# Zero-padded scan products, channel-major attention values and a new order for a hybrid decoder layer on one core

## The chip, the core and the metric

The kernel runs on one core of a Trainium2 chip. The core has five engines with a queue of instructions each: TensorE (PE in the profile; its weight loads are listed apart as PEld), VectorE (DVE), ScalarE (ACT), GpSimd (POOL) and SyncE (SP), whose queue starts the transfers. An engine works through its queue in order, and the engines wait for one another by semaphores. Matmuls read SBUF and write PSUM. The metric is the device time of one execution in microseconds (us); lower is better.

## The reference

One layer over 512 tokens of 1024 channels. What matters here are two mixers that run on the same projection of the normalized input.

```python
P = h @ W_in                       # attention q/k/v, scan inputs, gate logits
# attention: groups of (window, dilation); per head the groups are
# weighted by their softmax denominators (lse)
wts = softmax(stack(lses), axis=0)
y_att = sum(wts[..., None] * stack(outs), axis=0) @ W_att_out
# RWKV-7: for every token, with a 64x64 state for each of 16 heads
sa = state @ aa_t
state = state * w_t + sa * bb_t + v_t * k_t
y_t = state @ r_t
# then
x = x + gate1 * ((sig(g_att) * y_att + sig(g_rwkv) * y_rwkv) @ W_o)
x = x + gate2 * ConvFFN(adaLN(RMSNorm(x), c))
out = RMSNorm(x)
```

The conditioning vector `c` gives six rows of scales, shifts and gates: `c @ w_ada + b_ada`.

## The kernel before

Nearly all large products are made in three passes, as high times high, high times low and low times high parts of weights and activations. A weight block is loaded into a `raw` tile (two buffers), ACT copies its high part to `whi` (L1141, L193), DVE subtracts to get `wlo` (L1144, L194), and TensorE then runs 512-column matmuls (all through the helper at L148; transposes at L151). In the trace a product of plain 32-bit operands is two matmul instructions with two weight loads, so the counts of small products there are twice those of the calls.

**A planner sets the order.** From the start to the end of the scan (about 0 to 750 us) the order of each engine's queue isn't the order of the code. `Plan.add` takes a task with its engine, an estimated time, a priority, what it depends on, which buffers it takes and gives, and a `lag`: a time for which, after the engine is free again, the task's result and buffers still count as not there. `Plan.run` simulates all engines with these estimates and issues the tasks in the simulated order. On the chip each engine follows that order, however long things really take. Large projections (`body`, one task for each matmul) have low priority and fill TensorE between other tasks.

**Attention (`attention`, L672).** In two halves of four heads, first for the group with dilation 1 (`gi` 0), then for the group with dilation 4 (`gi` 1). `attend` (L788) goes through blocks of 128 queries of a pair of heads: `scores` on TensorE, `stat` (mask and minimum) on DVE, `exp` on ACT, `turn` (transposes) on TensorE, `turned` (copy to `pts`, two buffers), `values` (L831) on TensorE into `po`, and `out` (L841), a copy to `o[gi]`. There are 28 blocks with two key blocks and 4 with one. `values` makes tokens the rows of the result: the probabilities are the stationary operand (128x128), and 64 columns of the values move. When all is done, the two groups' shares are worked out (`diff`, `exps`, `share`, L1000 to L1013), `scale` (L1015) multiplies the rows of `o` by them, `turn` transposes the two groups into the same PSUM tile so that they add up, ACT copies it (L1034) and SP stores it to `att_d`. The second group's tokens are interleaved by 4, and the transposes write them back in order. Only when all these tasks are done is the memory of the next stage opened (`opened`).

**Conditioning (`ada_rest`, L328).** Four of the six rows are made in the same stretch: 8 loads of 512 KB each into `araw` (two buffers), 8 multiply-adds on DVE into `acc` (L345, L347), and then small matmuls named `ada` that sum over the rows of `acc`.

**Scan.** Sixteen heads go in four groups `g` of two pairs. `pair` (L1228) makes keys, rates and so on of two heads, `inverse` (L1441) or `inverse16` (L1577) solves a group's triangular blocks, and `chain` (L1745) carries the state through eight blocks `c` of 64 tokens. A chain step has these groups on TensorE: `state` (L1798), that is `xy<-mbd,ar` (for `c` > 0) and then four products `xy<-uv,gt` over the 64 rows of one half; `state_out`, `xo<-mbd,ar`; `solve`, `u<-xs,gt`; `update`, `u<-uv,bkt`; and `outs`, `xo<-uv,gt`. Every second block, `vals` adds `u<-cen,v` and two ACT copies into `uv`. `inverse` inverts 32x32 blocks on DVE in 14 double and 3 single steps; `inverse16` inverts 16x16 blocks in 6 double and 3 single steps, and joins them with two TensorE passes (`half_pe`, L1679) of 64 products of 32x32 tiles each. Groups 0 to 2 use `inverse`, group 3 `inverse16`. Memory for the pairs of group `g` is that of group `g`-2.

**Output product (`rwkv_out`, L2098).** Behind the plan comes code in program order. `rwkv_out` goes through eight blocks `m` of output channels, each 24 matmuls `pr` (blocks 0 to 2 have 18 of them done ahead). The weights of blocks 3 and 4 are loaded ahead, those of 5 to 7 when the block two before is done. In the same loop DVE and ACT mix the branches (`mhi`, `mlo`), and one row block of `w_o` is loaded and split in each turn, through the same two `raw` buffers. Then come the product with `w_o` (`mix_out`, matmuls `o`) and the gated MLP.

Of the kernel before, what the change touches and what calls it, by code (L numbers as in the profile page):

```python
# [10 lines left out]
F32 = mybir.dt.float32  # L11
F32R = mybir.dt.float32r
# [6 lines left out]
P = 128  # L19
S = 512  # L20
# [108 lines left out]
class Layer:  # L129
# [198 lines left out]
    def ada_rest(self):  # L328
# [5 lines left out]
        for part, name in ((2, "gt1"), (3, "sh2"), (4, "sc2"), (5, "gt2")):  # L334
            d, prev = {}, None
            for k in range(KD):
                def load(k=k, d=d, part=part):
                    d["raw", k] = self.accp.tile([P, D], F32, tag="araw", name=self.n("araw"), bufs=2)
                    nc.sync.dma_start(d["raw", k], self.w_ada[0][k * P : (k + 1) * P, part * D : (part + 1) * D])

                def step(k=k, d=d):
                    raw, ck = d["raw", k], self.col["c"][:, k : k + 1]
                    if k == 0:
                        d["acc"] = self.accp.tile([P, D], F32, tag="acc", name=self.n("acc"), bufs=2)
                        nc.vector.tensor_scalar(d["acc"], raw, ck, 0.0, op0=ALU.mult, op1=ALU.add)  # L345
                    else:
                        nc.vector.scalar_tensor_tensor(d["acc"], raw, ck, d["acc"], op0=ALU.mult, op1=ALU.add)  # L347
# [324 lines left out]
    def attention(self):  # L672
# [4 lines left out]
        o = [ap.tile([P, 4, ATT_W], F32, name="o0"), None]  # L677
# [110 lines left out]
        def attend(gi, hf, order, blocks, width, mask, V, ready, prio):  # L788


            last, pos, scs = {0: [], 1: []}, {}, []
            S0, E0 = S_ + prio, E_ + prio
            for n, i, new, end in order:
# [37 lines left out]
                def values(n=n, i=i, d=d, new=new, end=end):  # L831
                    if new:
                        pos[n] = self.aps.tile([P, 256], F32, tag="po", name=self.n("po"), bufs=2)
                    vs = V(n)
                    for h in range(2):
                        cs = slice(i * P + h * 64, i * P + h * 64 + 64)
                        for j, v in enumerate(vs):
                            self.mm(pos[n][:, cs], d["pts"][:, h, j * P : (j + 1) * P], v[:, cs],
                                    new and h == 0 and j == 0, end and h == 1 and j == len(vs) - 1)

                def out(n=n, i=i, new=new):  # L841
                    c0, c1 = (i * P if new else 0), i * P + P
                    if gi and o[1] is None:
                        o[1] = ap.tile([P, 4, ATT_W], F32, tag="o1", name="o1")
                    nc.scalar.copy(o[gi][:, n, hf * 256 + c0 : hf * 256 + c1], pos[n][:, c0:c1])
# [11 lines left out]
                t = pe(0.9 * wd / 256, values, [t], S0, take=("po",) if new else (), give=("pts",), name="po")  # L857
                last[i].append(t)
                if end:
                    first = gi and not outs[gi]  # L860
                    outs[gi].append(sca(0.37, out, [t], E0, take=("o1",) if first else (), give=("po",), name="o"))
# [106 lines left out]
        for _ in ada:  # L968
            pass

# [23 lines left out]
        scaled = []  # L994
        for gi in range(2):
# [19 lines left out]
            def scale(n, gi=gi, ea=ea):  # L1015
                ov = o[gi][:, n, :].rearrange("p (h e) -> p h e", h=8)
                nc.vector.tensor_tensor(ov, ov, ea[:, n, :].unsqueeze(2).to_broadcast([P, 8, 64]), op=ALU.mult)
            t = dve(0.6, diff, [got[gi], *stats[gi]], name="al")
            t = sca(0.45, exps, [t], name="al")
            t = dve(1.2, share, [t], name="al")  # L1020
            scaled += [dve(0.7, lambda n=n, scale=scale: scale(n), [t, *outs[gi]], name="al") for n in range(4)]
        for i in range(4):
            d = {}

            def turn(i=i, d=d):
                d["pa"] = self.aps.tile([P, S], F32, tag="pt", name=self.n("pa"), bufs=2)
                for n in range(4):
                    self.tr(d["pa"][:, n * P : (n + 1) * P], o[0][:, n, i * P : (i + 1) * P], n == 0, False)
                for n in range(4):
                    self.tr(d["pa"][:, n::4], o[1][:, n, i * P : (i + 1) * P], False, n == 3)  # L1030

            def out(d=d):
                d["t"] = self.awl.tile([P, S], F32, tag="attT", name=self.n("attT"), bufs=2)
                nc.scalar.copy(d["t"], d["pa"])  # L1034
            t = pe(0.95, turn, scaled, take=("pt",), name="pa")
            t = sca(0.6, out, [t], take=("attT",), give=("pt",), name="pa")
# [540 lines left out]
    def inverse16(self, g):  # L1577
# [101 lines left out]
        def half_pe(j):  # L1679

            if j == 0:
                d["pe"] = self.cps.tile([P, 512], F32, tag="t", name=self.n("pe"))
            for y in range(16):
# [61 lines left out]
    def chain(self, g):  # L1745
# [24 lines left out]

        def value(c, x):
            if x == 0:
                uvs[c] = cw.tile([P, 2, 256], F32, tag="uv", name=self.n("uv"), bufs=2)
# [9 lines left out]
        def vals(c):  # L1783
            t = pe(0.54, lambda: values(c), [start, last_uv])
            t = sca(0.38, lambda: value(c, 0), [t], C_, take=("uv",))
            uvd[c] = uvd[c + 1] = sca(0.38, lambda: value(c, 1), [t], C_)
        vals(0)
        for c in range(NCH):
# [9 lines left out]
            def state(c=c, s=s, gt=gt, R=R, X=X, ih=ih):  # L1798
# [4 lines left out]
                for i, h, cs, ci in ih:  # L1803
                    self.mm(xy[X[i], cs], gt(i, h, R[i], X[i]), s["uv"][R[i], ci], c == 0 and h == 0, h == 1)
# [45 lines left out]
            st = pe(0.6 if c else 0.33, state, [uvd[c], start] + mb, take=("xy",), name=f"xy{g}.{c}")  # L1850
            so_ = pe(0.33 if c else 0.0, state_out, [st], C_ + 0.01, take=("xo",), name="xo")
# [246 lines left out]
    def rwkv_out(self, mpool, wpool, psp):  # L2098
# [16 lines left out]
        for m in range(KD):  # L2115
# [3 lines left out]
            if 2 < m < KD - 2:  # L2119
                ahead.append(block(m + 2))  # L2120
# [284 lines left out]
```

## Time and profile before

| | |
|---|---|
| three runs | 1211.57, 1217.01, 1217.90 us (median 1217.01) |
| profiled execution | 1212.94 us, span 1211.2 us |
| mean granted TensorE clock | 0.993 |
| TensorE instructions | 7456 matmuls, 7456 weight loads |
| ACT / POOL instructions | 1014 / 228 |
| DMA | 138.39 MB, mean 114 GB/s |

The profile is of one execution. A row of the timeline has the start of an instruction (or of a run of like ones), its time, the engine, the line, the operation, the tile written and the tiles read, the shapes and the count; a bracket gives the idle time before it and what ended it. For matmuls the shapes begin with the rows and columns of the array that are in use, as in 128*64. A matmul's own time is its latency; how often one can start is seen from the next start. A row of a group has the count, the busy time and the mean of one in ns, then the idle time before it. In rows of waits the three numbers are the total, how often, and the longest.

### The profile page before, as it was taken

Reading aid. Unit: us, or ns where it says so; the run is one execution under the profiler, and the core shown is the slowest. Engines: PE = TensorE matmul, PEld = TensorE weight load, DVE = VectorE, ACT = ScalarE, POOL = GpSimd, SP = SyncE. Lnnn points to the kernel's source line nnn. Section 1 sums busy time; section 2 is a strip of 40 time slices with the busy share of each in tenths; the row PEclk is TensorE's granted clock in tenths of the full one; section 3 lists DMA queues with packets and bytes.
Section 4 is the critical chain, followed back from the end, with each engine's and each line's share of the span. In section 5 each row is a group of like instructions: output and inputs, shape, how many; then the busy total and the mean of one; then the engine's idle time right before and its main releaser. Section 6 shows DMA issues by size and latency. Waiting matters only on the chain.

```text
span 1211.2 us, 18982 instructions
## 1 busy us (share of the span) xinstructions
PE 1170.6 (97%) x7456; PEld 945.9 (78%) x7456; DVE 737.5 (61%) x1248; ACT 542.3 (45%) x1014; POOL 108.6 (9%) x228
## 2 busy tenths in 40 slices
PE   4999998999999999999999999999999999999997
PEld 3788887889777776767787667788888888888886
DVE  5688862431668986855797564764566665652235
ACT  4475521622565555364636453444444444441223
POOL 4000000000000103122102222003000000000001
PEclk9999999999999999999999999999999999999999
DMA  9845871130143342422332335460233333332331
GB/s 316 257 131 171 280 223 56 53 91 18 23 135 95 83 115 78 122 74 75 87 97 86 117 94 159 155 209 18 70 97 94 104 88 105 89 117 93 103 122 70
DMA packets 168040, 138.39 MB, mean 114 GB/s; under 512 B 8753, under 2 KB 150155, under 8 KB 167951
## 3 DMA queue, kind: packets, MB, share of 16 engines
q1 hardware_dynamic: 167807, 136.93, 37.2%
q8 instruction: 58, 0.95, 0.3%
q14 instruction: 31, 0.25, 0.1%
q10 hardware_dynamic: 144, 0.26, 0.1%
HBM read 127.13 MB, written 10.04 MB: 113 GB/s over the span
## 4 chain that ended last, share of the span: by engine, by line
PE 81%; DVE 8%; DMA 6%; ACT 2%; issue 2%; SPq 0%; POOL 0%; POOLq 0%; DVEq 0%; ACTq 0%
PE u L148 22%; PE o L148 13%; PE v L148 7%; PE pg L148 7%; PE qk L148 6%; PE r L148 3%; DMA araw<-in_w_ada_dram 3%; PE k L148 3%; PE pa L148 2%; PE early L148 2%; PE po L148 2%; PE xy L148 2%; PE pr L148 2%; PE xo L148 2%; PE pt L151 1%
## 5 line engine op out<-in xcount | busy, mean ns | idle before, releaser
L194 DVE TENSOR_TENSOR wlo<-raw,whi 128x1024 fp32r<-128x1024 f32 x65 | 79.6, 1225 | 141.1 <-ACT whi L193 141.1
L148 PE MATMUL u<-h2hi,whi 128*128 128x512 f32 (+2 forms) x368 | 140.6, 382 | 0.0
L148 PE MATMUL u<-h2lo,whi 128*128 128x512 f32 (+2 forms) x368 | 140.6, 382 | 0.0
L148 PE MATMUL u<-h2hi,wlo 128*128 128x512 f32 (+2 forms) x368 | 140.5, 382 | 0.0
L1141 ACT CAST whi<-raw 128x1024 fp32r<-128x1024 f32 (+2 forms) x73 | 72.6, 994 | 119.6 <-PE qk L148 45.5
L193 ACT CAST whi<-raw 128x1024 fp32r<-128x1024 f32 x65 | 68.5, 1054 | 97.3 <-PE o L148 53.7
L1144 DVE TENSOR_TENSOR wlo<-raw,whi 128x1024 fp32r<-128x1024 f32 (+2 forms) x73 | 83.7, 1148 | 19.5 <-ACT whi L1141 19.3
L148 PEld LDWEIGHTS u<-h2hi,wlo 128*128 128x128 f32 x368 | 69.1, 188 | 13.2
L148 PEld LDWEIGHTS u<-h2hi,whi 128*128 128x128 f32 x368 | 69.1, 188 | 13.2
L148 PEld LDWEIGHTS u<-h2lo,whi 128*128 128x128 f32 x368 | 69.1, 188 | 13.2 <-POOL h2lo L405 0.2
L2231 DVE SCALAR_TENSOR_TENSOR u<-u,cols,u 128x511 f32<-128x511 f32 x88 | 65.7, 746 | 4.5 <-ACT u L2229 3.0
L148 PE MATMUL qk<-hhi,wlo 128*128 128x512 f32 x160 | 64.0, 400 | 0.0
L148 PE MATMUL qk<-hhi,whi 128*128 128x512 f32 x160 | 63.6, 398 | 0.0
L148 PE MATMUL qk<-hlo,whi 128*128 128x512 f32 x160 | 63.6, 397 | 0.0
L148 PE MATMUL o<-whi,fhi 128*128 128x512 f32 x144 | 56.1, 390 | 0.3 <-DVE u L2231 0.3
L148 PE MATMUL o<-whi,flo 128*128 128x512 f32 x144 | 56.0, 389 | 0.0
L148 PE MATMUL o<-wlo,fhi 128*128 128x512 f32 x144 | 56.0, 389 | 0.0
L148 PE MATMUL pg<-hlo,whi 128*128 128x512 f32 x128 | 52.0, 406 | 0.0
L148 PE MATMUL pg<-hhi,whi 128*128 128x512 f32 x128 | 51.6, 403 | 0.0
L148 PE MATMUL pg<-hhi,wlo 128*128 128x512 f32 x128 | 51.5, 403 | 0.0
L810 DVE CUSTOM_DVE_ANT_0 sm<-sc,m 128x256 f32<-128x256 f32 (+1 forms) x64 | 23.9, 404 | 37.6 <-PE sc L148 36.5
L347 DVE SCALAR_TENSOR_TENSOR acc<-araw,cols,acc 128x1024 f32<-128x1024 f32 x28 | 35.9, 1281 | 17.3 <-DMA araw<-in_w_ada_dram 17.1
(450 smaller groups left out, 2761.3 us busy)
## 6 DMA issues: line engine op xcount, KB each, us to landing
raw<-in_w_in_dram SPq DMA_DIRECT2D x62, 512.0 KB
raw<-in_w_up_dram SPq DMA_DIRECT2D x44, 512.0 KB
araw<-in_w_ada_dram SPq DMA_DIRECT2D x32, 512.0 KB
raw<-in_w_down_dram SPq DMA_DIRECT2D x22, 512.0 KB
araw<-in_w_ada_dram SPq DMA_DIRECT2D x32, 256.0 KB
wvraw<-in_w_in_dram SPq DMA_DIRECT2D x20, 256.0 KB
raw<-in_w_rwkv_out_dram SPq DMA_DIRECT2D x8, 512.0 KB
raw<-in_w_o_dram SPq DMA_DIRECT2D x8, 512.0 KB
```

Source lines behind the costliest of these rows:

```text
L148: return self.nc.tensor.matmul(out, lhsT, rhs, start=start, stop=stop)
L151: self.nc.tensor.matmul(out, in_, self.ident[: in_.shape[0], : in_.shape[0]], is_transpose=True, start=start, stop=stop,)
L193: self.nc.scalar.copy(hl[0], raw)
L194: (lo_eng or self.nc.vector).tensor_tensor(hl[1], raw, hl[0], op=ALU.subtract)
L347: nc.vector.scalar_tensor_tensor(d["acc"], raw, ck, d["acc"], op0=ALU.mult, op1=ALU.add)
L810: nc.vector.tensor_tensor_reduce(d["sm", h][:, :wd], d["sc"][h][:, :wd], m[:, 256 - wd : 256] if gi == 0 else m[:, :wd], 1.0, 3.0e38, op0= ...
L1141: nc.scalar.copy(d["w"][0], d["raw"])
L1144: nc.vector.tensor_tensor(d["w"][1], d["raw"], d["w"][0], op=ALU.subtract)
L2231: nc.vector.scalar_tensor_tensor(u[:, d:], pu[:, : S - d], ch(c), u[:, d:], op0=ALU.mult, op1=ALU.add)
```

## The change

Seven edits, none of which changes what is computed:

1. `attend`: `values` makes channels the rows of the result. The values' 64 columns of a head are stationary, the 128 probabilities move, and the two heads write the two halves of PSUM's rows; the loop over heads is the inner one. Two blocks form one TensorE task (`got`), with a planned time of 0.05 us and 0.45 us for a full block, each, where it was 0.9 us a block. `out` stores channel-major.
2. Joins: the shares (128 tokens x 8 heads) are transposed, split into high and low rows (`share`), and spread over the channels by a product with `heads`, a 40-row table of ones and zeros made once by POOL (`share_rows`). DVE multiplies `o` by the result from PSUM, one group and channel block at a time, and POOL adds the two groups, reading the second in its interleaved order.
3. `ada_rest`: the last multiply-add of each row gets a `lag` of 3.0 us in the plan.
4. Group 0 uses `inverse16` too.
5. `half_pe` is cut into four tasks of 16 products, planned with 0.45 us and a `lag` of 0.4 us each, where it was one task of 2.6 us.
6. `state`: the products `xy<-uv,gt` run over all 128 rows; POOL first fills the other halves of `uv` with zeros (`zero`). The planned times of `state` and `state_out` go from 0.6 and 0.33 to 0.5 and 0.24 us.
7. `rwkv_out`: the weights of blocks 5 to 7 are loaded in turns 1 to 3 instead of 3 to 5.

```diff
@@ ada_rest
-                              give=("araw2",), name="ada")
+                              give=("araw2",), lag=3.0 if k == KD - 1 else 0.0, name="ada")
@@ attention
+    def share_rows(self):
+        nc = self.nc
+        self.heads = self.awl.tile([P, 2, S], F32R, tag="qk12", name="heads", bufs=1)[:40, 0, :]
+        t = self.awl.tile([P, 2, S], F32R, tag="qk02", name="share", bufs=1)[:40]
+        self.share = [t[:, gi, :] for gi in range(2)]
+        one = lambda r, c: self.ident[r, c : c + 8].unsqueeze(2).to_broadcast([r.stop - r.start, 8, 64])
+        h = self.heads.rearrange("p (h e) -> p h e", e=64)
+        for r, c in ((slice(0, 32), 0), (slice(32, 40), 32)):
+            nc.gpsimd.tensor_copy(h[r], one(r, c))
+        for x in self.share:
+            nc.gpsimd.tensor_copy(x[:32].rearrange("p (h e) -> p h e", e=64), one(slice(0, 32), 64))
@@ attend
-                    for h in range(2):
-                        cs = slice(i * P + h * 64, i * P + h * 64 + 64)
-                        for j, v in enumerate(vs):
-                            self.mm(pos[n][:, cs], d["pts"][:, h, j * P : (j + 1) * P], v[:, cs],
-                                    new and h == 0 and j == 0, end and h == 1 and j == len(vs) - 1)
+                    for j, v in enumerate(vs):
+                        for h in range(2):
+                            c0 = i * P + h * 64
+                            self.mm(pos[n][h * 64 : h * 64 + 64, i * P : i * P + P], v[:, c0 : c0 + 64],
+                                    d["pts"][:, h, j * P : (j + 1) * P], new and j == 0, end and j == len(vs) - 1)
...
-                t = pe(0.9 * wd / 256, values, [t], S0, take=("po",) if new else (), give=("pts",), name="po")
+                got.append((t, values, out, new, end, i, 0.05 + 0.45 * wd / 256))
+                if len(got) < 2:
+                    continue
+                t = pe(sum(x[-1] for x in got), lambda fs=[x[1] for x in got]: [f() for f in fs], [x[0] for x in got], S0,
+                       take=("po",) * sum(x[3] for x in got), give=("pts", "pts"), name="po")
...
+            def turn(gi=gi, d=d):
+                d["ps"] = self.aps.tile([P, S], F32, tag="pt", name=self.n("pe"), bufs=2)
+                for n in range(4):
+                    self.tr(d["ps"][:8, n * P : (n + 1) * P], shares[gi][1][:, n, :], n == 0, n == 3)
+            def hi(gi=gi, d=d):
+                nc.scalar.copy(self.share[gi][:8], d["ps"][:8])
+            def lo(gi=gi, d=d):
+                nc.vector.tensor_tensor(self.share[gi][32:40], d["ps"][:8], self.share[gi][:8], op=ALU.subtract)
...
+            def turn(gi, i=i, d=d):
+                d["w", gi] = self.aps.tile([P, S], F32, tag="pt", name=self.n("pw"), bufs=2)
+                self.mm(d["w", gi], self.heads[:, i * P : (i + 1) * P], self.share[gi], True, True)
+            def scale(gi, i=i, d=d):
+                nc.vector.tensor_tensor(o[gi][:, i, :], o[gi][:, i, :], d["w", gi], op=ALU.mult)
+            def out(i=i, d=d):
+                d["t"] = self.awl.tile([P, S], F32, tag="attT", name=self.n("attT"), bufs=2)
+                nc.gpsimd.tensor_tensor(d["t"], o[0][:, i, :], o[1][:, i, :].rearrange("p (r j) -> p j r", r=4), op=ALU.add)
@@ rwkv
-            (self.inverse16 if g in (3,) else self.inverse)(g)
+            (self.inverse16 if g in (0, 3) else self.inverse)(g)
@@ inverse16
-            t = pl.add("PE", 2.6, lambda j=j: half_pe(j), [t, ey], 0.5, take=() if j else ("t",), name="pe")
+            for q in range(4):
+                t = pl.add("PE", 0.45, lambda j=j, q=q: half_pe(j, q), [t, ey], 0.5, take=() if j + q else ("t",), lag=0.4, name="pe")
@@ chain
+        def zero(c):
+            uvs[c] = cw.tile([P, 2, 256], F32, tag="uv", name=self.n("uv"), bufs=2)
+            for x in range(2):
+                b = uvs[c].rearrange("p x (i n) -> p (x i) n", i=2)[64 * x : 64 * x + 64]
+                nc.gpsimd.memset((b[:, 0:4:3] if x else b[:, 1:3]), 0.0)
...
-                    self.mm(xy[X[i], cs], gt(i, h, R[i], X[i]), s["uv"][R[i], ci], c == 0 and h == 0, h == 1)
+                    self.mm(xy[X[i], cs], gt(i, h, slice(0, P), X[i]), s["uv"][:, ci], c == 0 and h == 0, h == 1)
...
-            st = pe(0.6 if c else 0.33, state, [uvd[c], start] + mb, take=("xy",), name=f"xy{g}.{c}")
-            so_ = pe(0.33 if c else 0.0, state_out, [st], C_ + 0.01, take=("xo",), name="xo")
+            st = pe(0.5 if c else 0.33, state, [uvd[c], start] + mb, take=("xy",), name=f"xy{g}.{c}")
+            so_ = pe(0.24 if c else 0.0, state_out, [st], C_ + 0.01, take=("xo",), name="xo")
@@ rwkv_out
-            if 2 < m < KD - 2:
-                ahead.append(block(m + 2))
+            if 0 < m < KD - 4:
+                ahead.append(block(m + 4))
```

More of the change, by code (lines that the diff above doesn't have):

```diff
@@ L788, in attend @@
         def attend(gi, hf, order, blocks, width, mask, V, ready, prio):
-            last, pos, scs = {0: [], 1: []}, {}, []
+            last, pos, scs, got = {0: [], 1: []}, {}, [], []
             S0, E0 = S_ + prio, E_ + prio
@@ L856, in attend @@
                 t = (dve if i else sca)(0.68 if wd == 256 else 0.42, turned, [t], E0, take=("pts",), give=("pt",), name="pts")
-                t = pe(0.9 * wd / 256, values, [t], S0, take=("po",) if new else (), give=("pts",), name="po")
[L858 to L861, printed above, removed]
+                got.append((t, values, out, new, end, i, 0.05 + 0.45 * wd / 256))
[3 more added lines that the diff above has]
+                       take=("po",) * sum(x[3] for x in got), give=("pts", "pts"), name="po")
+                for _, _, out, _, end, i, _ in got:
+                    last[i].append(t)
+                    if end:
+                        first = gi and not outs[gi]
+                        outs[gi].append(sca(0.37, out, [t], E0, take=("o1",) if first else (), give=("po",), name="o"))
+                got = []
             return last, scs
@@ L969, in attention @@
             pass
+        heads = pl.add("POOL", 3.0, self.share_rows, sc, E_, take=("qk02", "qk12"), name="heads")
         def pre():
@@ L993, in attention @@
                    oth[1].rearrange("p n a h -> p n (a h)"), st_d[0].rearrange("(p n) f -> p n f", n=4)), [st[0]], W_, lag=2.0)]
-        scaled = []
+        shares = []
         for gi in range(2):
@@ L1013, in share @@
                 nc.vector.tensor_tensor(ea, ea, dn, op=ALU.mult)
-            def scale(n, gi=gi, ea=ea):
-                ov = o[gi][:, n, :].rearrange("p (h e) -> p h e", h=8)
-                nc.vector.tensor_tensor(ov, ov, ea[:, n, :].unsqueeze(2).to_broadcast([P, 8, 64]), op=ALU.mult)
             t = dve(0.6, diff, [got[gi], *stats[gi]], name="al")
             t = sca(0.45, exps, [t], name="al")
-            t = dve(1.2, share, [t], name="al")
-            scaled += [dve(0.7, lambda n=n, scale=scale: scale(n), [t, *outs[gi]], name="al") for n in range(4)]
+            shares.append((dve(1.2, share, [t], name="al"), ea))
@@ new lines, in attention @@
+        parts = []
+        for gi in range(2):
+            d = {}
+            def turn(gi=gi, d=d):
[6 more added lines that the diff above has]
+                nc.vector.tensor_tensor(self.share[gi][32:40], d["ps"][:8], self.share[gi][:8], op=ALU.subtract)
+            t = pe(0.48, turn, [shares[gi][0], heads], take=("pt",), name="pa")
+            t = sca(0.6, hi, [t], name="pa")
+            parts.append(dve(0.7, lo, [t], give=("pt",), name="pa"))
@@ L1022, in attention @@
         for i in range(4):
             d = {}
[L1025 to L1032, printed above, removed]
-                d["t"] = self.awl.tile([P, S], F32, tag="attT", name=self.n("attT"), bufs=2)
-                nc.scalar.copy(d["t"], d["pa"])
@@ new lines, in out @@
+            def out(i=i, d=d):
+                d["t"] = self.awl.tile([P, S], F32, tag="attT", name=self.n("attT"), bufs=2)
+                nc.gpsimd.tensor_tensor(d["t"], o[0][:, i, :], o[1][:, i, :].rearrange("p (r j) -> p j r", r=4), op=ALU.add)
+            ts = []
+            for gi in range(2):
+                t = pe(0.24, lambda gi=gi, turn=turn: turn(gi), [parts[gi]], take=("pt",), name="pa")
+                ts.append(dve(0.7, lambda gi=gi, scale=scale: scale(gi), [t, *outs[gi]], give=("pt",), name="pa"))
@@ L1037, in attention @@
+            t = pl.add("POOL", 1.2, out, ts, E_, take=("attT",), name="pa")
             pl.add("DMA", 0.8, lambda i=i, d=d: nc.sync.dma_start(self.att_d[:, i, :], d["t"]), [t], W_, lag=2.0,
@@ L1677, in rows11, with half_pe @@
             nc.vector.transpose(d["t11"], d["tc"])
-        def half_pe(j):
-            if j == 0:
+        def half_pe(j, q):
+            if j + q == 0:
                 d["pe"] = self.cps.tile([P, 512], F32, tag="t", name=self.n("pe"))
-            for y in range(16):
+            for y in range(4 * q, 4 * q + 4):
                 for e, b, x in quads:
@@ L1784, in vals @@
             t = pe(0.54, lambda: values(c), [start, last_uv])
-            t = sca(0.38, lambda: value(c, 0), [t], C_, take=("uv",))
+            z = pl.add("POOL", 0.6, lambda: zero(c), [start], C_, take=("uv",))
+            t = sca(0.38, lambda: value(c, 0), [t, z], C_)
             uvd[c] = uvd[c + 1] = sca(0.38, lambda: value(c, 1), [t], C_)
```

13 lines of the change are left out of this document (5 added, 8 removed).

## The prediction

> **What bounds the kernel.** I read the page's busy shares and its chain that ended last, then the stretches by engine, then TensorE's timeline wherever a stretch was not full.
>
> ```profile
> span 1211.2 us, 18982 instructions
> PE 1170.6 (97%) x7456; PEld 945.9 (78%) x7456; DVE 737.5 (61%) x1248; ACT 542.3 (45%) x1014; POOL 108.6 (9%) x228
> PE 81%; DVE 8%; DMA 6%; ACT 2%; issue 2%; SPq 0%; POOL 0%; POOLq 0%; DVEq 0%; ACTq 0%
> ```
>
> TensorE is busy 97% of the span and is 81% of the chain. But "busy" counts pipelined matmuls by their latency, so costs have to be read from one start to the next. In the longest stretch of the chain that is:
>
> ```profile
> 846.36 236.78 PE u L148 x1073
> ```
>
> 236.78/1073 = 0.22 us for a 512-column matmul. Time is won by issuing less on TensorE, or by removing the places where it stands still. The stretches (columns: length; busy time of PE, PEld, DVE, ACT, POOL; granted clock; DMA) show such places:
>
> ```profile
> 180.00:200.00 20.00, 16.27 (x60) 12.76 (x59) 9.17 (x12) 1.64 (x2) 1.17 (x5) 0.91 0.38 110
> 350.00:435.00 85.00, 84.73 (x451) 68.19 (x450) 76.20 (x132) 45.96 (x72) 4.97 (x10) 1.00 0.35 97
> 682.00:700.00 18.00, 15.32 (x466) 11.59 (x465) 6.84 (x12) 8.84 (x23) 2.36 (x5) 0.91 0.16 47
> 746.00:793.00 47.00, 44.63 (x196) 35.20 (x195) 31.50 (x42) 18.33 (x23) 1.82 (x3) 0.96 0.46 141
> ```
>
> Three of them have idle time and a clock below 1. If the clock is either 1 or one half, it was halved for 0.09x20/0.5 = 3.6, 3.2 and 3.8 us, some 3.5 us each; half of that, 1.7 us, is lost besides the wait itself.
>
> **Attention values.** Today a block is eight instructions of 64 moving columns; the change makes them 128 columns on half the array's columns, the heads alternating, two blocks in one visit. The nearest rows of that form are the scan's `u<-cen,v`.
>
> ```profile
> 313.27 1.00 PE L148 MATMUL po<-v,pts 128*128 128x64 f32 x8
> 314.11 0.61 PE L151 MATMUL pt<-ident,pr 128*128 128x128 f32 x4
> ```
> ```profile
> L148 PE MATMUL po<-v,pts 128*128 128x64 f32 x240 | 30.6, 269 | 0.8 <-DVE pts L829 0.8
> ```
> ```profile
> 443.64 0.66 PE L148 MATMUL u<-cen,v 128*64 128x128 f32 x8
> 444.23 0.50 PE L148 MATMUL pg<-hhi,whi 128*128 128x512 f32 x1
> 444.57 0.40 PE L148 MATMUL pg<-hlo,whi 128*128 128x512 f32 x1
> ```
> ```profile
> 455.71 0.61 PE L148 MATMUL u<-cen,v 128*64 128x128 f32 x8
> 456.15 0.40 PE L148 MATMUL xo<-uv,gt 128*64 128x64 f32 x8
> ```
>
> Before: 240/8 = 30 units of 0.84 = 25.2 us. After: eight such instructions take 0.44 us between neighbours of their own shape, which is 0.11 a pair, so the halves overlap. Between wide matmuls they take 0.59, and the wide one behind them 0.34 instead of 0.22; with as much again on entry I count 0.80. There are 12 visits of 16 instructions (0.80+0.44) and 4 of 12 (0.80+0.22): 19.0 us. **-6.2 us**. Ends: 30x0.44 = 13.2 (-12.0) if no visit pays for a change of shape; 240x0.11 plus 16x0.2 = 29.6 (+4.4) if the halves, which here have different moving operands, do not overlap.
>
> **Keys' products over all rows.** The second group of the scan's step goes from 64x64 tiles to 128x64, the shape of its neighbours; the other rows of the values are zero.
>
> ```profile
> 521.88 0.45 PE L148 MATMUL u<-uv,bkt 128*64 128x64 f32 x8
> 522.16 0.40 PE L148 MATMUL xo<-uv,gt 128*64 128x64 f32 x8
> ```
> ```profile
> 524.09 0.44 PE L148 MATMUL xy<-mbd,ar 128*64 128x128 f32 x4
> 524.46 0.45 PE L148 MATMUL xy<-uv,gt 64*64 64x64 f32 x8
> 524.84 0.44 PE L148 MATMUL xo<-mbd,ar 128*64 128x128 f32 x4
> 525.21 0.50 PE L148 MATMUL r<-hlo,whi 128*128 128x512 f32 x1
> ```
>
> The three groups take 1.12 us today. Two pairs of 128 columns are 0.22 us, twice; eight instructions of 64 columns are 0.28 with an entry of 0.05, so 0.23; entry 0.05, exit 0.10: 0.82 after. There are 4x7 steps with a carried state: 28x0.30 = 8.4; I take **-8.0**, and -7.0 to -8.4 as ends.
>
> [...] The trace does not agree that row tiles pay here: the group of eight took 0.38 us in row tiles, its like in full rows (522.16) 0.34.
>
> The zeros are two POOL fills for each of 16 pairs of blocks. POOL is 9% busy and the fills need only a free buffer: nothing. Bare, they would cost at most what POOL's larger operation below does, 16x0.78 = 12 us.
>
> **Joins.** Thirty-two transposes become eight short ones and eight wide products; DVE keeps eight scalings of the same size, now out of PSUM, and POOL adds four 128x512 sums in place of four ACT copies.
>
> ```profile
> L151 PE MATMUL pa<-ident,o 128*128 128x128 f32 x32 | 3.9, 275 | 0.2 <-DVE o L1017 0.2
> ```
> ```profile
> L1976 POOL TENSOR_TENSOR yt<-yt,var 128x256 f32<-128x256 f32 x16 | 12.5, 779 | 1.3
> ```
>
> TensorE: 3.9 against 8x0.34 and some 0.8: **-0.4**. The path to the stored result gains a copy, a subtraction and a POOL sum of about 1.6 us and loses a copy: some 2 us later. Behind it wait the first loads of the next stage; 48 wide matmuls (11 us) of the first pair can run meanwhile. Nothing, with 2 us as the end.
>
> **Inverses.** Block 16 for the first group adds two passes of 128 tiny matmuls. The only pass seen is the fourth group's:
>
> ```profile
> 686.31 1.26 PE L148 MATMUL pe<-lr,gt 32*32 32x16 f32 x128
> 687.50 0.44 PE L148 MATMUL xy<-mbd,ar 128*64 128x128 f32 x4
> ```
> ```profile
> 689.17 1.26 PE L148 MATMUL pe<-lt,lr 32*32 32x16 f32 x128 [0.48 <-issue]
> 692.62 0.45 PE L148 MATMUL u<-xs,gt 64*64 64x64 f32 x8 [2.19 <-issue]
> ```
>
> A pass is 1.19 us; around the second, TensorE stands 0.48 and 2.19 us with nothing to wait for ("issue"), as if instructions ran out after 128 in 1.2 us. Quarters, with other work between, should not empty the queue: 0.30 us and 0.25 of entry and exit, eight of them 4.4 us. First group **+4.4** (2.4 to 6.4, the upper end with such a wait and half the clock loss again). Fourth: 2x1.19+0.48+2.19+1.7 = 6.75 falls to 4.4, **-2.4**. DVE is spared eight of fourteen two-column steps where it is 76 of 85 us busy (350 to 435 us), but TensorE is full there: nothing in itself; it keeps the chains from becoming the bound.
>
> **Waits planned apart.** `ada` products are queued before their sums exist:
>
> ```profile
> 183.22 0.39 PE L148 MATMUL v<-wvhi,hlo 128*128 128x512 f32 x1
> 186.91 1.02 PE L148 MATMUL ada<-acc,few 128*1 128x256 f32 x4 [3.30 <-DVE acc L347]
> ```
>
> Three microseconds more in the plan put other work there: 3.3+1.7 = **-5.0**. What is late next is again this sum if TensorE gets there sooner (first rival).
>
> [...]
>
> **Weights of the output product.** Blocks 5 to 7 are requested two products earlier.
>
> ```profile
> 771.71 0.39 PE L148 MATMUL pr<-yhi,w 128*128 128x512 f32 x1
> 773.70 0.50 PE L148 MATMUL pr<-yhi,whi 128*128 128x512 f32 x1 [1.60 <-ACT whi L193]
> ```
> ```profile
> 793.11 0.39 PE L148 MATMUL o<-wohi,mhi 128*128 128x512 f32 x1
> ```
> ```profile
> 768.77 0.38 SPq L178 DMA_DIRECT2D raw<-in_w_rwkv_out_dram  x1
> ```
>
> From 771.71 to 793.11 are 21.4 us for 73 wide matmuls, 16.1 us of work: 5.3 lost, half clock included. Block 5 is requested at 768.77, and TensorE wants it 3 us later; two loads sooner is enough. In ACT's queue the split of block 7 now waits for product 5, with the mixing of block 3 and four splits of `w_o` behind it; the next stage needs those only from about 788. **-5.0**, 0 if that pile-up starves it.
>
> **Sum**: -6.2-8.0-0.4+4.4-2.4-5.0-5.0 = -22.6. The profiled execution took 1212.9 us (span 1211.2 and 1.7 around it); the three runs have their median 4 us above. From halfway, 1215: **1192 us**. A measurement of this kernel can tell about 0.5%.
>
> **Rivals.**
>
> 1. The `ada` sums come no sooner, being bound by loads, and TensorE arrives earlier by what the first half's values save (112 of 240 instructions, 2.9 us): 1192+5.0+2.9 = 1200. For it: the wait has no slack; against: 3 us of planned distance. 0.13.
> 2. The chains set the end, not TensorE:
>
> ```profile
> 755.95 1.46 DVE L2078 TENSOR_TENSOR ylo<-y,yhi 128x512 fp32r<-128x512 f32 x2
> ```
> ```profile
> 756.89 0.40 PE L148 MATMUL pr<-yhi,whi 128*128 128x512 f32 x1
> ```
>
> TensorE turns to the last two rows of y just as they are done (757.41), so there is no slack. If the path through pairs, inverses and chains gets no shorter, 8.0+2.4-4.4 = 6.0 us are lost: 1198. 0.13.
>
> 3. The column halves of the values do not overlap: +10.6, 1203. Against it stand the 0.11 us pairs. 0.08. That eight products in full rows take twice the 0.23 us of a step, the two row halves no longer side by side: 28x0.23 = 6.4 more, 1198; 0.04. That the clock is halved without these waits too: 3x1.7 = 5.1 more, 1197; 0.05.
> 4. It does not do what it says: the plan's order changes everywhere and brings as many such standstills as it removes, three or four of 5 us: 1210. 0.07.
> 5. **Slower**: the plan also holds a load buffer 3 us longer at the end of each `ada` part, and SP's queue, in order, puts weight loads behind loads that wait for such a buffer.
>
> ```profile
> SPq L339 <- DVE acc L347: 31.0, 19, 9.5
> ```
> ```profile
> ACT whi L1141 <- PE qk L148: 45.5, 13, 6.2
> ```
>
> Thirteen times ACT waited for TensorE to free a weight buffer, 3.5 us each: that is the lead of the weights. If each came 6 us later, TensorE would stand 13x2.5 = 32 us: 1224. It turns slower than before from about 5.6 us on. 0.05.
>
> **Numbers.** The forecast holds 0.45. The range reaches from 1181 (values and quarters at their good ends, with 1 us beyond) to 1206, which takes in the rivals at 1197 to 1203; outside stay the last two and the tails. Faster by over 0.5%: forecast, rivals 1 to 3, less the tails, 0.86; within 0.5%: 0.09; slower: 0.05.
>
> **What would show it.** Right: visits of 16 `po` instructions near 1.0 us; the three scan groups near 0.82 us with no 64*64 group; no wait over 1 us before `ada` and none for issue behind the quarters; `pr` at 0.22 us throughout; clock 1.00 in the three stretches. Wrong: TensorE waiting for `ada` sums, for weights between 100 and 190 us, or for the last rows of y, or `po` pairs 0.22 us apart.

## The result, and the profile after

The changed kernel takes **1203.3 us** (median of 6 runs, 1200.8 to 1204.5) against 1216.7 us (6 runs, 1211.6 to 1220.5) for the kernel before: ratio 0.989, 95% interval 0.986 to 0.992. It is faster by 13 us, about 1%. The forecast was 1192 us with a range of 1181 to 1206: the sign and the range hold, the forecast is 11 us too low. The two profiled executions differ by less (spans 1211.2 and 1202.5 us, 8.7 us), as the profiled one of before was 4 us faster than its median.

The page of the changed kernel, in the same rows as before:

```profile
span 1202.5 us, 19533 instructions
...
PE 1165.9 (97%) x7696; PEld 932.7 (78%) x7696; DVE 730.4 (61%) x1231; ACT 545.4 (45%) x1015; POOL 123.1 (10%) x268
...
PE 88%; DVE 6%; ACT 2%; DMA 2%; issue 1%; SPq 0%; POOL 0%; POOLq 0%; DVEq 0%; ACTq 0%
```

TensorE has 240 instructions more, and it is 88% of the chain where it was 81%. The stretches (length; busy time of PE, PEld, DVE, ACT, POOL; granted clock; DMA):

```profile
180.00:200.00 20.00, 20.00 (x84) 18.10 (x84) 8.50 (x11) 2.81 (x4) 1.13 (x4) 1.00 0.35 105
320.00:340.00 20.00, 18.57 (x65) 12.97 (x65) 11.30 (x18) 6.47 (x11) 6.17 (x5) 0.83 0.33 99
...
660.00:690.00 30.00, 29.68 (x599) 21.24 (x599) 17.01 (x32) 19.18 (x45) 7.54 (x15) 1.00 0.60 190
740.00:760.00 20.00, 15.71 (x59) 12.37 (x58) 15.68 (x21) 9.30 (x11) 0.00 (x0) 0.83 0.58 171
760.00:785.00 25.00, 25.00 (x112) 20.69 (x111) 14.46 (x19) 8.43 (x10) 0.00 (x0) 1.00 0.34 114
```

The three stretches that were to be mended are mended: before the `ada` sums (180 to 200), around the fourth group's inverse (660 to 690) and in the last products `pr` (from 760) the clock is 1.00 and TensorE is full. Two stretches are new, 320 to 340 and 740 to 760, each with a clock of 0.83: 0.17x20/0.5 = 6.8 us at half clock, twice as long as each of the old ones. What stands in them is in the timeline. The first is the joins:

```profile
322.15 0.49 PE L148 MATMUL pw<-share,heads 40*128 40x512 f32 x1
322.57 0.50 PE L148 MATMUL k<-hlo,whi 128*128 128x512 f32 x1
322.91 0.40 PE L148 MATMUL k<-hhi,wlo 128*128 128x512 f32 x1
323.23 0.49 PE L148 MATMUL pw<-share,heads 40*128 40x512 f32 x1
...
325.18 0.49 PE L148 MATMUL pw<-share,heads 40*128 40x512 f32 x1
...
327.10 0.80 PE L148 MATMUL r<-hhi,whi 128*128 128x512 f32 x1 [1.43 <-DVE lt L1193]
```

A round of one `pw` and two wide matmuls takes 1.08 us, and the two wide ones alone would take 0.45: a `pw` costs 0.63 us. Behind the last one TensorE waits for DVE. The second place is in the output product:

```profile
750.12 0.40 PE L148 MATMUL pr<-yhi,w 128*128 128x512 f32 x1
...
751.76 1.04 ACT L193 CAST whi<-raw 128x1024 fp32r<-128x1024 f32 x1 [1.35 <-DMA raw<-in_w_rwkv_out_dram]
752.84 1.23 DVE L194 TENSOR_TENSOR wlo<-raw,whi 128x1024 fp32r<-128x1024 f32 x1 [1.10 <-ACT whi L193]
753.98 1.28 DVE L2168 SCALAR_TENSOR_TENSOR gate<-gate,pr 128x512 f32<-128x512 f32 x2
...
754.81 0.77 PE L148 MATMUL o<-wohi,mhi 128*128 128x512 f32 x1 [4.29 <-DVE gate L2168]
755.37 0.63 PE L148 MATMUL o<-wolo,mhi 128*128 128x512 f32 x1
755.80 0.63 PE L148 MATMUL o<-wohi,mlo 128*128 128x512 f32 x1
756.22 0.63 PE L148 MATMUL pr<-yhi,w 128*128 128x512 f32 x1
```

Three products of `mix_out`, which belong behind all `pr`, stand between blocks 2 and 3 (the code behind the plan isn't issued strictly in program order, as the text on the kernel put it). They wait for `gate`, DVE's reading of an earlier `pr`; DVE does that only after the split `wlo` of block 5, whose weights have just arrived. That is 4.5 us of standstill and 3.4 us lost to the clock.

Two steps of the prediction that can be read in the same trace. A visit of the values, and a scan step:

```profile
310.25 1.09 PE L148 MATMUL po<-pts,v 128*64 128x128 f32 x16
311.27 0.41 PE L148 MATMUL lg<-hhi,wlo 128*32 128x512 f32 x1
...
494.86 0.44 PE L148 MATMUL xy<-mbd,ar 128*64 128x128 f32 x4
495.13 0.40 PE L148 MATMUL xy<-uv,gt 128*64 128x64 f32 x8
495.36 0.39 PE L148 MATMUL xo<-mbd,ar 128*64 128x128 f32 x4
495.68 0.50 PE L148 MATMUL pg<-hlo,whi 128*128 128x512 f32 x1
```

Sixteen value instructions take 1.02 us, and the three groups of the step 0.82 us, where it was 1.12.

### The profile page after: what moved, and what is told of

Its sections match the earlier page's. It is cut to its first block, busy times and chain, and to the rows that moved or that the text cites. A ratio compares the mean times of both kernels' runs of the same rounds, so it can differ in the third digit from the quotient of the medians.

```text
span 1202.5 us, 19533 instructions
## 1 busy us (share of the span) xinstructions
PE 1165.9 (97%) x7696; PEld 932.7 (78%) x7696; DVE 730.4 (61%) x1231; ACT 545.4 (45%) x1015; POOL 123.1 (10%) x268
## 4 chain that ended last, share of the span: by engine, by line
PE 88%; DVE 6%; ACT 2%; DMA 2%; issue 1%; SPq 0%; POOL 0%; POOLq 0%; DVEq 0%; ACTq 0%
PE u L148 22%; PE o L148 13%; PE qk L148 9%; PE v L148 8%; PE pg L148 8%; PE r L148 4%; PE k L148 4%; PE pr L148 2%; PE pa L148 2%; PE early L148 2%; PE xy L148 2%; PE pt L151 2%; PE sc L148 2%; PE po L148 1%; DMA raw<-in_w_rwkv_out_dram 1%; PE xo L148 1%
```

## The experiments

Each set of four kernels ran on one chip, together with the kernel before. Medians are of 4 runs (10 for attention_of_before, 5 for lt_ahead_of_joins); the span is that of the profiled execution.

| kernel | median us | span us | ratio to before, 95% interval |
|---|---|---|---|
| changed kernel | 1203.3 | 1202.5 | 0.989 (0.986 to 0.992) |
| o_behind | 1199.9 | 1198.3 | 0.989 (0.986 to 0.992) |
| shares_128_rows | 1199.2 | 1196.5 | 0.989 (0.985 to 0.992) |
| both_mended | 1193.3 | 1191.7 | 0.983 (0.981 to 0.986) |
| o_behind_old_weights | 1201.9 | 1199.2 | 0.990 (0.987 to 0.993) |
| group0_by_inverse | 1202.7 | 1199.5 | 0.990 (0.987 to 0.992) |
| keys_half_rows | 1203.0 | 1201.4 | 0.990 (0.986 to 0.993) |
| attention_of_before | 1208.4 | 1206.2 | 0.996 (0.994 to 0.998) |
| heads_outer | 1195.6 | 1192.0 | 0.984 (0.981 to 0.986) |
| lt_ahead_of_joins | 1209.2 | 1203.8 | 0.994 (0.992 to 0.997) |
| group1_by_16_too | 1200.5 | 1198.7 | 0.987 (0.985 to 0.990) |
| ada_without_lag | 1194.9 | 1192.5 | 0.982 (0.980 to 0.985) |
| whole_passes | 1200.6 | 1200.4 | 0.987 (0.984 to 0.990) |

The kernel before had medians of 1214.1 to 1216.7 us in the four sets, so differences of under some 3 us between kernels of different sets are read from the traces, not from the medians. The changed kernel is a set by itself; the rows behind it are three sets of four, in this order.

**o_behind.** The three `o` products are put behind the last `pr`; nothing else moves on TensorE.

```diff
-            prod(w, pr, range(late if m < 3 else 0, KD))
+            self.pr_last = prod(w, pr, range(late if m < 3 else 0, KD))
...
             if n == 0:
-                part(range(KD), 0, 1)
+                with self.tc.issue_after(self.pr_last.ins):
+                    part(range(KD), 0, 1)
```

> The changed kernel, with the three products o<-wohi,mhi that stand between blocks 2 and 3 of the output product put behind its last block; nothing else in TensorE's queue moves. Theory A: these three wait for a PSUM buffer that DVE's gate reads free, DVE reads late because the split of block 5 stands ahead of them, and all of blocks 3 to 7 queue behind. Then the 4.7 us gap at 750 us goes and with it the 6.8 us at half clock: 8.1 us less, about 1195 us, no wait over 1 us between 740 and 780 us. Theory B: DVE's lateness (block 5 requested early) is the cause and the next user of a buffer or of the mixed rows waits as long: within 2 us of the changed kernel, 1201 to 1203.

The stand at 750 us is gone, with its half clock (mean clock of the execution 0.992, where the changed kernel had 0.990). In the traces, which agree to 0.5 us up to the last `xo` (730.5 and 731.0 us), the last `pr` starts 6.7 us sooner (784.8 and 778.1). But the span is only 4.2 us shorter, since the stage behind gives some back. In TensorE's timeline of o_behind:

```profile
797.13 0.39 PE L148 MATMUL o<-wohi,mlo 128*128 128x512 f32 x1
798.77 1.27 PE L151 MATMUL tr<-ident,xn 128*128 128x128 f32 x8 [1.25 <-ACT xn L2237]
```

TensorE comes to the first transposes of `xn` before ACT and DVE are through, and the three `o` products (0.7 us) now lie in that stage. Theory A holds for the stand, and 2.5 us of the 6.7 are late elsewhere. The changed kernel ran in another set: against it o_behind is 3.4 us shorter by the medians and 0.4 by the ratios, so this rests on the traces.

**shares_128_rows and both_mended.** The shares and the table of ones get 88 rows of zeros, so that `pw` contracts 128 rows.

```diff
-        self.heads = self.awl.tile([P, 2, S], F32R, tag="qk12", name="heads", bufs=1)[:40, 0, :]
-        t = self.awl.tile([P, 2, S], F32R, tag="qk02", name="share", bufs=1)[:40]
+        self.heads = self.awl.tile([P, 2, S], F32R, tag="qk12", name="heads", bufs=1)[:, 0, :]
+        t = self.awl.tile([P, 2, S], F32R, tag="qk02", name="share", bufs=1)
...
-        for r, c in ((slice(0, 32), 0), (slice(32, 40), 32)):
+        for r, c in ((slice(0, 32), 0), (slice(32, 64), 32), (slice(64, 128), 0)):
             nc.gpsimd.tensor_copy(h[r], one(r, c))
         for x in self.share:
-            nc.gpsimd.tensor_copy(x[:32].rearrange("p (h e) -> p h e", e=64), one(slice(0, 32), 64))
+            for r, c in ((slice(0, 64), 64), (slice(64, 128), 0)):
+                nc.gpsimd.tensor_copy(x[r].rearrange("p (h e) -> p h e", e=64), one(r, c))
```

> The changed kernel with the products pw of the joins over 128 rows (the 88 added rows are zeros), so the array is used in the same form as by the wide products around. Theory A: 40 rows make TensorE change its form twice for each product, which is why a pw costs 0.63 us more in the stream instead of the 0.34 I took; then it falls to about 0.23, 8 x 0.4 = 3.2 us, and the wait of 1.4 us for lt with its half clock (3.4 us) goes too if DVE keeps up: 1195 to 1200 us. Theory B: the cost is the hand-over with DVE through the two buffers (each pw waits for a scaling of 0.69 us plus 0.4 us): then pw stays 1.09 us apart and the time stays at 1203 us.

> Both edits: the o products behind the last block and pw over 128 rows. If both theories A hold the gains add, being 420 us apart: 8.1 + 3.2 to 8.0 us less than the changed kernel, 1187 to 1192 us, which is what I forecast for the change. If only one holds, 1195 to 1200 us.

The joins in the timeline of both_mended:

```profile
319.72 0.39 PE L148 MATMUL pw<-share,heads 128*128 128x512 f32 x1
319.95 0.39 PE L148 MATMUL k<-hhi,wlo 128*128 128x512 f32 x1
320.18 0.39 PE L148 MATMUL k<-hhi,whi 128*128 128x512 f32 x1
...
320.41 0.39 PE L148 MATMUL pw<-share,heads 128*128 128x512 f32 x1
...
324.23 0.50 PE L148 MATMUL r<-hhi,whi 128*128 128x512 f32 x1 [1.45 <-DVE lt L1194]
```

A `pw` is now 0.23 us like its neighbours, and the round 0.69. Theory A holds: a product of 40 rows cost 0.4 us more than one of 128. The extra time lies on both sides of a change of shape: in the changed kernel the wide matmul ahead of a `pw` takes 0.32 us, the `pw` 0.42 and the wide one behind it 0.34, where each takes 0.23 with full rows. The wait of 1.4 us for `lt` stayed, against theory A's hope, as DVE now does its eight scalings without a break and `lt` comes behind them; but in this trace no half clock followed it (clock 1.00 from 315 to 345 us). In one set, both_mended is 6.7 us below o_behind and 5.9 below shares_128_rows, so each edit gains when the other is in place. Against the changed kernel, which ran in another set, it is 10.8 us shorter by the spans and 7.1 by the ratios; how nearly the gains add is known only to that. It is 21.4 us below the kernel before in its own set, where 22.6 was forecast for the change, and 1 us above the 1187 to 1192 expected here.

**o_behind_old_weights.** As o_behind, with blocks 5 to 7 requested in turns 3 to 5.

```diff
-            if 0 < m < KD - 4:
-                ahead.append(block(m + 4))
+            if 2 < m < KD - 2:
+                ahead.append(block(m + 2))
```

> As o_behind, but the weights of blocks 5 to 7 requested in turns 3 to 5 as before the change. It prices that edit alone, without the three products. Theory A (my term of -5.0): TensorE waits again some 1.6 and 0.5 us for block 5 and runs 3.4 to 6.8 us at half clock, 4 to 5.5 us above o_behind: about 1199 us. Theory B: the early request is worth nothing or costs, since splits of w_o queue behind it: within 1 us of o_behind or below it.

TensorE's timeline in the last products:

```profile
770.16 0.39 PE L148 MATMUL pr<-yhi,wlo 128*128 128x512 f32 x1
772.91 0.50 PE L148 MATMUL pr<-yhi,whi 128*128 128x512 f32 x1 [2.37 <-ACT whi L193]
773.25 0.40 PE L148 MATMUL pr<-ylo,whi 128*128 128x512 f32 x1
774.36 0.50 PE L148 MATMUL pr<-yhi,wlo 128*128 128x512 f32 x1 [0.71 <-DVE wlo L194]
```

The old waits are back. From the last `xo` to the last `pr`, with as many matmuls in it, it takes 52.1 us instead of 47.1: 5.0 us, the size forecast. The stage behind is 1.8 us shorter than in o_behind, since less has piled up, so the end sees some 3.2 us by the traces and 2.0 by the medians. (The spans differ by only 0.9, as this run came to the last `xo` 2.2 us sooner.) Theory A, less what is given back.

**group0_by_inverse.** From here on, each kernel is both_mended with one thing undone or added.

```diff
-            (self.inverse16 if g in (0, 3) else self.inverse)(g)
+            (self.inverse16 if g in (3,) else self.inverse)(g)
```

> both_mended with group 0 solved by blocks of 32 again, as before the change. Theory A (my term): blocks of 16 cost TensorE eight visits of 0.58 us and give it nothing, since it is full in that stage; undone, 4.5 us less: 1188 to 1189 us. Theory B: the eight DVE steps that they spare let the first chain start earlier, and DVE, 90% busy there, becomes the bound without them: 1194 us or more, and TensorE waits for DVE before the first chain.

It is 7.8 us slower in span and 9.4 in median: theory B by its time. The first chain's first solve in TensorE's timeline of both_mended:

```profile
428.42 0.45 PE L148 MATMUL u<-xs,gt 64*64 64x64 f32 x8
```

The same in group0_by_inverse, 7.3 us later, and the end of its scan:

```profile
435.71 0.45 PE L148 MATMUL u<-xs,gt 64*64 64x64 f32 x8
...
738.81 0.28 PE L148 MATMUL xo<-uv,gt 128*64 128x64 f32 x2
739.02 0.55 PE L151 MATMUL t<-ident,yt 128*128 128x128 f32 x3
742.42 0.48 PE L151 MATMUL t<-ident,yt 128*128 128x128 f32 x1 [2.85 <-POOL yt L2023]
743.96 1.09 PE L151 MATMUL t<-ident,yt 128*128 128x128 f32 x4 [1.06 <-DVE y L1985]
747.06 1.22 PE L148 MATMUL pr<-yhi,whi 128*128 128x512 f32 x2 [2.02 <-ACT yhi L2124]
```

The last chain ends at 738.9 us instead of 724.9. The cost does not show where the work was saved, but 300 us later: TensorE has run out of other work and waits for the last rows of y, 5.9 us in three stands, with a clock of 0.86 over 720 to 750 us. The wait for DVE before the first chain, which theory B also named, is not there: from 350 to 435 us TensorE has no stand over 0.6 us.

**group1_by_16_too.** The list of groups is (0, 1, 3).

> both_mended with blocks of 16 for group 1 as well. Undoing it for group 0 cost 9 us, since the chains ran late and TensorE had nothing else at the end of the scan. Theory A: with group 0 mended TensorE is full until the last chain (no wait above 0.7 us from 345 to 772 us), so another group only adds its eight visits of 0.58 us: 4 to 5 us more, 1197 to 1198 us. Theory B: DVE's steps still hold the chains of group 1 back, and an earlier end of the chains wins more: 1193 us or less.

1200.5 us, 4.5 us more than both_mended by the ratios and 7.0 by the spans: theory A, with two new waits of 1.4 us each (for `cs` and for a `wlo`) in the larger figure. Blocks of 16 pay for group 0, whose chain is first, and not for group 1 as well.

**keys_half_rows.** The four products `xy<-uv,gt` use `R[i]` again, and `zero` is left out.

> both_mended with the keys' products over the 64 rows of one half again and without the zeros. Theory A (my term of -8.0; the traces of before and after show 34.1 and 27.0 us for the three groups): 7 to 8 us more, 1200 to 1201 us. Theory B: products in full rows save nothing that the end sees, since the chains' own path sets it: within 2 us of both_mended.

7.5 us more by the ratios, 9.7 by the spans: theory A, a little above its price. In the traces the three groups take 33.2 us instead of 27.0. Two new stands are in the larger figure, 1.2 us for a `wlo` and this one, inside a quarter of 32 instructions (from TensorE's waits: total, times, longest):

```profile
PE pe L148 <- issue: 1.2, 1, 1.2
```

**attention_of_before.** `attention` and `attend` are those of the kernel before.

> both_mended with the attention of before: values token-major, one block at a time, joins by transposes. Values cost 25.0 us in place of 15.5 in the traces; the joins' TensorE time 3.9 in place of some 3.2, but the wait of 1.5 to 1.9 us for lt behind the scalings goes. Theory A: 9.5 + 0.7 - 1.9, about 8 us more: 1201 us. Theory B: the joins in their new form still delay the first pair behind them: 5 us more or less, 1198 us.

14.5 us more in span, where 8 were expected. Some 10 us are TensorE's own: the `po` instructions take 25.0 us from start to start instead of 15.5, and the joins' transposes some 1 us more than the new products with full rows. The rest is spread: 1.8 us lost to a clock of 0.91 between 415 and 435 us, waits of 1.9 and 0.7 us for weights in `pr`, 1.4 for `gs`. Neither theory had these.

**heads_outer.**

```diff
-                    for j, v in enumerate(vs):
-                        for h in range(2):
+                    for h in range(2):
+                        for j, v in enumerate(vs):
```

> both_mended with the loop over heads outside the loop over key blocks in the values, so that two instructions for the same half of the array's columns follow one another, where they alternate now. Theory A: halves with different operands run side by side only as neighbours; a visit of 16 then has pairs for the same half, twice the time at those places, and the values go from 15.5 to 20 us or more: 1198 to 1203 us. Theory B: an instruction of 128 columns streams at 0.065 us whatever its neighbour: 1193 us.

The same visit of the values in its timeline:

```profile
310.42 1.14 PE L148 MATMUL po<-pts,v 128*64 128x128 f32 x16
...
311.50 0.42 PE L148 MATMUL lg<-hhi,wlo 128*32 128x512 f32 x1
```

A visit takes 1.08 instead of 1.02 us, the span 0.3 us more (2.0 if the 1.7 us of one stretch of half clock are added, which this run has less of: its mean clock is 0.997, that of both_mended 0.996): theory B by its time. That neighbours alternate between the heads is not what makes the values cheap. Whether the two halves run side by side is not decided by it: within such a merged row the single instructions of the changed kernel start in pairs, 7 ns apart and then some 103 ns to the next pair (120 pairs in the 16 visits), and here 72 of the 240 still start within 20 ns of the one before.

**ada_without_lag.**

```diff
-                              give=("araw2",), lag=3.0 if k == KD - 1 else 0.0, name="ada")
+                              give=("araw2",), name="ada")
```

> both_mended without the 3 us that the plan adds to the last multiply-add of each ada row. Theory A (my term of -5.0): TensorE waits 3 us for acc again with one or two windows of half clock behind it: 4.7 to 6.4 us more, 1198 to 1200 us. Theory B: with the attention shorter the order differs anyway and the wait does not come back: 1193 us.

The place of the old wait in its timeline:

```profile
186.29 1.02 PE L148 MATMUL ada<-acc,few 128*1 128x256 f32 x4 [0.37 <-DVE acc L347]
```

0.4 us of wait in place of 3.3, no half clock (the wide matmuls behind it start 0.23 us apart again), and 0.8 us in the span: theory B. With the new attention the wait does not come back without the lag; attention_of_before, which has the lag and the old attention, has no such wait either. Either edit is enough.

**whole_passes.** `half_pe` runs its 64 products in one task again, for both groups.

> both_mended with the two passes of the inverses from blocks of 16 uncut, 128 tiny instructions in a run, for groups 0 and 3. Theory A (my reading of before): each pass takes 1.19 us and leaves TensorE without instructions for 0.5 and 2.2 us, against 2.3 us for four quarters; over four passes 2 x (2.4 + 2.7) against 9.3, 0.9 us more, and 1.7 to 3.4 us of half clock behind each longer stand: 1195 to 1201 us. Theory B: the stand of 2.2 us in before was of that place alone; whole passes then cost 2 x 2.4 + 2 x 0.3: 4 us less, 1189 us.

The passes of the fourth group in its timeline:

```profile
658.59 1.13 PE L148 MATMUL pe<-lr,gt 32*32 32x16 f32 x113
661.40 0.31 PE L148 MATMUL pe<-lr,gt 32*32 32x16 f32 x15 [1.69 <-issue]
...
662.91 1.51 PE L148 MATMUL pe<-lt,lr 32*32 32x16 f32 x102
664.86 0.60 PE L148 MATMUL pe<-lt,lr 32*32 32x16 f32 x26 [0.43 <-issue]
```

After 113 and 102 of 128 tiny instructions TensorE stands with nothing to wait for, in another place than before: theory A. It costs 4.1 us by the ratios, 8.7 by the spans; in the latter are also a wait of 3.6 us for a `whi` in `pr` and its half clock (0.91 from 765 to 785 us), which the new order brought.

**lt_ahead_of_joins.** An attempt at the wait that is left behind the joins: the scalings get a priority of `E_ + 0.5`.

> both_mended with DVE's scalings of the joins planned behind the steps that free the PSUM buffers of the lg and k products (lt stands ahead of seven of the eight scalings). Theory A: the wait of 1.5 us for lt behind the joins is DVE's order alone; it goes, 1.5 to 2 us less: 1191 to 1192 us. Theory B: the joins then end later and hold back the memory of the next stage; nothing won, 1193 to 1195 us.

The wait for `lt` is gone, and the kernel is 12.1 us slower in span. New among TensorE's waits (total, times, longest):

```profile
PE v L148 <- DVE k L1194: 3.4, 1, 3.4
...
PE v L148 <- ACT gs L2038: 2.9, 2, 1.7
PE v L148 <- DVE wlo L1184: 2.1, 1, 2.1
```

The plan behind that place comes out in another order on all engines, with new stands of up to 3.4 us and 10 us at half clock around 595 us (0.87 from 580 to 620 us). Neither theory foresaw it: 1.5 us won at the place, some 13 lost behind it.

## Why the prediction was right, and where it was wrong

In the traces of before and after, start to start, the terms came out so. They sum to about -7 against a difference of 8.7 us in the spans; the rest is spread over waits under 1 us.

| term | forecast | traces |
|---|---|---|
| values | -6.2 | -9.5, less 1.5 for 16 changes of shape ahead of the visits: -8.0 |
| keys' products | -8.0 | -7.1 (34.1 to 27.0 us in the three groups) |
| joins | -0.4 | +7: products 1.9, wait 1.5, half clock 3.4 |
| inverse, group 0 | +4.4 | +4.6 on TensorE |
| inverse, group 3 | -2.4 | -2.2 |
| `ada` wait | -5.0 | -5.2 |
| weights of the output product | -5.0 | +2.6 |
| start | 0 | +1.7: 6.8 us at half clock for 3.4, behind the same stand |

**The two steps that failed** are the joins and the weights. By the table they are 15 us worse than forecast, more than the 11 us by which the forecast was low, and with both mended the kernel takes 1193.3 us. That this is so near 1192 is partly luck: the values gained 1.8 us more than forecast, the start lost 1.7, and the sum held only as group 0 kept the chains early, for which it had no term. For the joins the step was "8x0.34": the price was taken from a wide product behind one of a different shape, but a product of 40 rows is itself of another shape than its neighbours and pays at both ends, 0.63 us. I had counted entry and exit for the small groups of the scan and not here. The step "nothing, with 2 us as the end" left out that DVE's `lt`, which frees TensorE's PSUM buffer, comes behind the scalings in DVE's queue.

For the weights, the working named "the mixing of block 3 and four splits" behind the split of block 7, and "0 if that pile-up starves it". The pile-up was real, but came two blocks sooner, at block 5's split, and in DVE's queue rather than ACT's; what it starved was not a `pr` at all but three `o` products that had got in front. I assumed that the order of `pr` and `o` on TensorE stays. In the programs as built, the three stand in front with blocks of 16 for group 0 and behind the last `pr` with `inverse` and all other edits; that version was not run, and why group 0 moves them is open. The edit by itself is worth what was forecast, 5.0 us in its stage, and 2 to 3 at the end.

**The values** gained more than forecast, since the change of shape was sized too high: a visit of 16 was put at 1.24 us, and it takes 1.02 and some 0.1 ahead of it. An instruction takes 0.064 us (1.02/16) instead of 0.105 (0.84/8). Why is not shown: one edit halved the stationary columns, doubled the moving ones and put the heads on two halves of the array, and no run separates these. One reading is the load of the stationary operand: an instruction took 105 ns where it loads 128 columns and 64 where it loads 64. But the eight `xy<-uv,gt` of the scan step above also load 64 columns each and take 0.23 us, 29 ns an instruction, so the load of one instruction after the other can't be the whole of it. The other reading is "the halves overlap" of the prediction; its 0.11 us a pair came out (7 and 103 ns, see heads_outer). So rival 3's first half, with its 10.6 us, did not come true. Its second half, full rows at twice the time, is out as well: the step's groups take the 0.82 us forecast, and with half rows the kernel takes 7.5 to 9.7 us more.

**Group 0** was priced right on TensorE (eight visits of 0.58 us), and the remark that the saved DVE steps (the edit "keeps the chains from becoming the bound") was the heart of it, though the sum held nothing for it. Undone, the kernel is not 4.5 us faster but 8 to 9 slower: without it rival 2 comes true, and part of what values and keys save is waited away at the end of the scan. Terms that shorten TensorE's work need the chains to come earlier by as much.

**The `ada` wait** went as forecast, but the lag isn't the reason: the shorter values move the plan far enough by themselves. **Group 3** came out as forecast, and whole_passes shows the stands for `issue` again. Quarters make them rarer but don't rule them out, as the one in keys_half_rows shows; both_mended has none.

**Rival 4**, as many standstills as the change removes, named what happened: two new ones for three old ones, each with twice the half clock. It had 0.07, with a price that was too high since it let everything come back.

## What to carry to other kernels

Price an operation by its neighbours: a matmul of 40 rows between wide ones cost two changes of shape here, and padding it with zeros to the neighbours' shape was cheaper (0.23 us instead of 0.63). When transfers or splits are asked for earlier, list for each in-order engine what now stands behind them and which buffer each of those frees; and look at the issued order again, since an edit far away can put other work in front. Work taken off the full engine only pays if the dependent chain gets shorter too (group0_by_inverse); undo one edit at a time from the best version, not from the first, to see what each is worth.

## What the runs showed of the hardware that wasn't expected

The same stand of 2.8 us near 33 us is in the traces of before and of the changed kernel, and brings 3.4 us at half clock in the one and 6.8 in the other. The stretch of 30 to 50 us in before:

```profile
30.00:50.00 20.00, 17.18 (x99) 14.86 (x98) 18.75 (x34) 10.22 (x15) 0.00 (x0) 0.91 0.89 265
```

The same in the changed kernel:

```profile
30.00:50.00 20.00, 17.17 (x88) 14.75 (x88) 18.05 (x33) 9.91 (x14) 0.00 (x0) 0.83 0.89 264
```

0.09 and 0.17 of 20 us, over one half, are 3.6 and 6.8 us. Over the same 20 us the clock is 0.83 in both_mended and 0.91 in o_behind_old_weights, so both values come with the change too. Inside the kernel, the half clock at its very end aside, before has four stretches at half clock of 3.4 us each, which begin up to 1.5 us behind the end of a stand; the changed kernel has three of 6.8 us each, and all three begin inside a stand. The stand of 1.4 us behind the joins has 6.8 us at half clock in the changed kernel and none in both_mended. Stands of 1.4 us (the joins) to 3.3 us (`ada` in before) had half clock behind them. In attention_of_before the clock was also halved with no stand of TensorE just ahead. From 415 to 435 us TensorE is busy all but 0.28 us, and that wait is at 431 us, while the wide matmuls that start 0.43 us apart, at half clock, lie ahead of 426 us:

```profile
415.00:435.00 20.00, 19.72 (x381) 14.93 (x383) 12.73 (x19) 13.93 (x24) 1.79 (x6) 0.91 0.28 73
```

What sets the clock there is open. A stand of this size thus cost its own length and 0, 1.7 or 3.4 us more, by luck as far as these runs show, and the 1.7 us that I put to each was the lower of two values that came.
